# Folding the memory keys into the query weights of a cross-attention, with the logits' second half as seven products of quarters

## The chip, the cores and the metric

The kernel runs on one core of one Trainium2 chip. The metric is the device time of one execution in microseconds (us), the median of several runs. The trace comes from the hardware profiler, for one execution.

## The reference

One layer of a streaming encoder over 1024 rows of 1024 numbers, in fp32: a mixing part with two groups of eight attention heads, a cross-attention with four heads into 256 memory rows, and a feed-forward part, each between two RMS norms. The change concerns the cross-attention and what lies around it:

```
def memory_cross_attention(h, mem_n, w_mq, w_mk, w_mv, w_mo):
    B, S, _ = h.shape
    M = mem_n.shape[1]
    q = (h @ w_mq).reshape(B, S, MEM_HEADS, MEM_HEAD_DIM)
    k = (mem_n @ w_mk).reshape(B, M, MEM_HEADS, MEM_HEAD_DIM)
    v = (mem_n @ w_mv).reshape(B, M, MEM_HEADS, MEM_HEAD_DIM)
    logits = jnp.einsum('bshd,bmhd->bhsm', q, k).astype(jnp.float32) * (MEM_HEAD_DIM ** -0.5)
    p = jax.nn.softmax(logits, axis=-1).astype(v.dtype)
    o = jnp.einsum('bhsm,bmhd->bshd', p, v).reshape(B, S, D_MODEL)
    return o @ w_mo
```

`h` is the RMS norm (gain `g_mem_pre`) of the rows behind the mixing part, `mem_n` that of the memory rows. Four heads of 256 dimensions, and 256 memory rows, so that the logits of one row are 1024 numbers.

## The kernel before

All products are made in three matmuls (`mm3`, L174 to L176): each factor is split into a high part, rounded to a shorter format, and a low part, which is the rest, and high x high, high x low and low x high are added in PSUM. In the names, `hi` and `lo` (or `h` and `l`) are these parts. ScalarE (ACT) makes the high part with a copy (L321 for the weights) and VectorE (DVE) or GpSimd the low part with a subtraction (L327, L330). Each matmul takes 128 rows by 128 columns of weights and 512 or 256 columns.

The order of the instructions is written by a planner, `Flow` (L56). Each engine (V, S, G, D for DVE, ACT, GpSimd and DMA issues) has a time at which it is next free; each instruction is put with a cost and a call that follows it; the products come as generators of steps, each with its cost on TensorE (PE) and a condition on tokens (`free`, buffers) and marks (`seen`, results). What the planner decides is the program order of each engine; on the chip each engine runs in that order and waits on semaphores. Loads and stores are issued by SyncE (SP), also in that order; the planner counts 0.55 us for the issue of one and a fixed time (2.5 to 6 us) until it is there.

The first phase (`attention_phase`, L1507) runs the attention of the mixing part, and fills PE's time with `filler_steps`: the projections of queries, keys and values, then `memory_key_steps` (`mk`, whose results are kept on the chip as `km`), then the output projection's first half, `mix_steps(0)`, and `memory_value_steps` (`mv`). `mix_steps` needs the attention output: a class `Outputs` (L947) loads it from DRAM (`oin<-od`, L995, four loads for 512 columns of one group), ACT and DVE split it (`yT_hi` L989, `yT_lo` L990), ACT squares it (L992) and DVE adds the squares into `sq` (L970), and `rstd_steps` (L1003) transposes the sums on PE (`ssh`, L1016), from which the group's row norms come. The products `yw` leave PSUM through ACT (`yt`, L1146, with the norm `rs` as scale) and go to DRAM (`yd`, L1148). In the names of this stage the first digit is the half of the tokens and the second the group: `oin100`, `oin010` and `oin110` follow one another, and `ssh01` belongs to `oin010`.

The second phase has `mix_steps(1)`, then the rows: `close_row` (L1061) adds the residual, takes the norm (DVE L1091 multiplies the row by its norm and by the gain `g_mem_pre`), and stores `x1d`; `row_steps` transposes and splits the rows (`h2T`). `query_steps` (L1213, `mq`) makes the queries, `memory_score_steps` (L1240, `ms`) the logits, per head, half of the tokens and block of 128 rows, with the largest value by a reduction on DVE (L1256), the exponential on ACT (L1258), and the division by the sum (L1261). `memory_turn_steps` transposes the probabilities, `memory_out_steps` multiplies by the values, and `product_quarters` and `product_steps` make the product with `w_mo`, the first half of the tokens in seven products of quarters (sums `wt` of `w_mo`, made ahead, stored and reloaded). The feed-forward part follows. Weights are loaded by `Stock` (L260) in a fixed list of blocks of 512 KB (`wraw`), when a raw buffer is free, and split when a home (`w`, `wq`, `u4`) is free.

## Time and profile before

| | us |
|---|---|
| median of 3 runs | 1451.21 (1451.16 to 1451.9) |
| the profiled execution | 1451.39 |
| its span in the trace | 1449.6 |
| PE busy | 1441.1 |
| DVE busy | 964.9 |
| ACT busy | 822.9 |
| GpSimd (POOL) busy | 386.6 |

The span is what the trace covers, from the first to the last recorded instruction; the execution took 1.8 us more. In a row of groups the columns are: line, engine, operation, output <- inputs, shape, count | busy us, mean ns of one | idle time of the engine just ahead of them, and what ended it. A timeline's row begins with the start and the length in us. PE clock is the share of full speed that the throttle granted. The DMA share is the mean busy share of the core's 16 DMA engines.

### The profile page before, as it was taken

To read this page: it belongs to the slowest core of one execution; us is meant where nothing else is said; L and a number is where in the kernel's file an instruction comes from. 1 tells how busy PE (TensorE), PEld (TensorE's weight loads), DVE (VectorE), ACT (ScalarE), POOL (GpSimd) and SP (SyncE) were. 2 spreads that over 40 slices of the span, in tenths; PEclk is the share of its full clock that TensorE was granted. 3 is DMA by queue.
4 is the path that set the end of the run, shared out by engine and by line. 5 is a ranking of instruction groups with operands and counts; after the bars stand their busy time and mean duration, and the time that the engine had idled before them with its cause. 6 is when DMAs were issued, how large, how long until landed. Compare 5 with 4: busy or idle time off the path is not lost.

```text
span 1449.6 us, 20870 instructions
## 1 busy us (share of the span) xinstructions
PE 1441.1 (99%) x7236; PEld 1220.1 (84%) x7236; DVE 964.9 (67%) x1650; ACT 822.9 (57%) x1466; POOL 386.6 (27%) x458
## 2 busy tenths in 40 slices
PE   9999999999999999999999999999999999999998
PEld 9888888888889888888888888888888888888886
DVE  5577778867667556966685697665555766655576
ACT  7457776666577664566665455545555453444442
POOL 1345555444344202300021504333331000000021
PEclk9999999999999999999999999999999999999999
DMA  8233567855538766542362646754444875445565
GB/s 336 69 100 92 145 166 192 276 124 126 131 95 246 217 211 234 190 156 71 118 204 71 206 159 233 262 180 160 160 157 163 299 302 197 136 148 187 185 251 203
DMA packets 100970, 259.44 MB, mean 179 GB/s; under 512 B 12520, under 2 KB 25072, under 8 KB 100864
## 3 DMA queue, kind: packets, MB, share of 16 engines
q1 hardware_dynamic: 96112, 249.71, 51.1%
q0 software_dynamic: 4608, 8.39, 4.1%
q8 instruction: 57, 0.93, 0.3%
q14 instruction: 49, 0.40, 0.1%
q10 hardware_dynamic: 144, 0.00, 0.0%
HBM read 181.98 MB, written 76.08 MB: 178 GB/s over the span
## 4 chain that ended last, share of the span: by engine, by line
PE 98%; DMA 0%; ACT 0%; DVE 0%; SPq 0%; issue 0%; DVEq 0%; POOLq 0%; POOL 0%; ACTq 0%
PE pv L636 4%; PE fx L175 4%; PE fx L174 4%; PE fx L176 4%; PE ptr L586 4%; PE px L176 3%; PE fy L174 3%; PE fy L175 3%; PE px L175 3%; PE px L174 3%; PE fy L176 3%; PE q L174 2%; PE q L175 2%; PE q L176 2%; PE mq L174 2%; PE yw L174 2%
## 5 line engine op out<-in xcount | busy, mean ns | idle before, releaser
L592 DVE TENSOR_TENSOR p<-ptr,p 128x512 fp32r<-128x512 f32 (+1 forms) x152 | 92.4, 616 | 31.6 <-ACT p L595 30.5
L2103 ACT ACTIVATE whif<-ra 128x1024 fp32r<-128x1024 f32 x37 | 39.2, 1061 | 127.0 <-PE fy L175 62.6
L2105 DVE TENSOR_TENSOR wlof<-ra,whif 128x1024 fp32r<-128x1024 f32 x37 | 45.3, 1225 | 89.4 <-ACT whif L2103 89.3
L595 ACT ACTIVATE p<-ptr 128x512 fp32r<-128x512 f32 (+1 forms) x152 | 79.8, 538 | 43.2 <-PE ptr L586 42.3
L2217 POOL TENSOR_SCALAR rf<-sf 128x1 f32<-128x1 f32 x8 | 8.3, 1032 | 324.7 <-ACT jf L2202 324.4
L636 PE MATMUL pv<-p,vs 128*128 128x512 f32 (+1 forms) x304 | 86.7, 372 | 0.0
L174 PE MATMUL fx<-vhif,whif 128*128 128x512 f32 x168 | 65.4, 389 | 0.0
L175 PE MATMUL fx<-vlof,whif 128*128 128x512 f32 x168 | 65.4, 389 | 0.0
L176 PE MATMUL fx<-vhif,wlof 128*128 128x512 f32 x168 | 65.4, 389 | 0.0
L636 PEld LDWEIGHTS pv<-p,vs 128*128 128x128 f32 x304 | 53.4, 189 | 8.7 <-DVE p L592 0.2
L1992 POOL TENSOR_TENSOR sc<-wf,wf 128x512 f32<-128x512 f32 x14 | 22.1, 1576 | 142.5 <-DMA wf<-in_w_ff 117.6
L174 PE MATMUL k<-hT_hi,whik 128*128 128x512 f32 x128 | 52.5, 411 | 0.0
L174 PE MATMUL mq<-h2T_hi,whimq 128*128 128x512 f32 x128 | 51.6, 403 | 0.0
L174 PE MATMUL q<-hT_hi,whiq 128*128 128x512 f32 x128 | 51.0, 398 | 0.0
L174 PE MATMUL yw<-whiwo,yT_hi 128*128 128x512 f32 x128 | 50.6, 395 | 0.0
L175 PE MATMUL k<-hT_lo,whik 128*128 128x512 f32 x128 | 50.2, 392 | 0.0
L176 PE MATMUL k<-hT_hi,wlok 128*128 128x512 f32 x128 | 50.2, 392 | 0.0
L175 PE MATMUL mq<-h2T_lo,whimq 128*128 128x512 f32 x128 | 50.1, 391 | 0.0
L175 PE MATMUL q<-hT_lo,whiq 128*128 128x512 f32 x128 | 50.1, 391 | 0.0
L176 PE MATMUL mq<-h2T_hi,wlomq 128*128 128x512 f32 x128 | 50.0, 391 | 0.0
L176 PE MATMUL q<-hT_hi,wloq 128*128 128x512 f32 x128 | 50.0, 391 | 0.0
L645 ACT ACTIVATE ot<-pv 128x512 f32<-128x512 f32 x64 | 37.8, 593 | 21.3 <-PE pv L636 21.1
(673 smaller groups left out, 4951.7 us busy)
## 6 DMA issues: line engine op xcount, KB each, us to landing
ra<-gd SPq DMA_DIRECT2D x56, 512.0 KB, 3.5
wg<-in_w_ff SPq DMA_DIRECT2D x56, 512.0 KB, 4.9
wf<-in_w_ff SPq DMA_DIRECT2D x38, 512.0 KB, 4.2
gd<-s SPq DMA_DIRECT2D x48, 256.0 KB, 2.1
od<-ot SPq DMA_DIRECT2D x64, 128.0 KB, 2.7
od<-od POOLq DMA_DIRECT2D x32, 256.0 KB, 4.9
wrawmq<-in_w_mq SPq DMA_DIRECT2D x16, 512.0 KB, 4.1
gd<-u SPq DMA_DIRECT2D x32, 256.0 KB, 2.0
```

The costliest lines, as they stand in the source:

```text
L174: nc.tensor.matmul(ps, lh, rh, start=start, stop=False, skip_group_check=more)
L175: nc.tensor.matmul(ps, lh, rl, start=False, stop=False, skip_group_check=more)
L176: nc.tensor.matmul(ps, ll, rh, start=False, stop=stop, skip_group_check=more)
L586: nc.tensor.transpose(tr[:, m, :], sp[:, k * P:(k + 1) * P], ident)
L592: flow.put("V", at, 0.56 if dead else 0.7, lambda: nc.vector.tensor_sub(pl[:, live, :], tr[:, live, :], f(ph[:, live, :])), done)
L595: flow.put("S", flow.end, 0.49 if dead else 0.6, lambda ph=ph, tr=tr, live=live: nc.scalar.activation(ph[:, live, :], tr[:, live, :], AF.C ...
L636: nc.tensor.matmul(pv[:, :, q0 * P:(q0 + k1 - k0) * P], v, x[:, :, k0:k1, :].rearrange("p m k q -> p m (k q)"), start=c == 0 and m == 0, s ...
L645: nc.scalar.activation(box["t"][:, :, :, ::step], pv.rearrange("p m (k q) -> p m k q", q=P), AF.Copy)
L1992: eng.tensor_sub(sc[:, k1], r0[:, k0], r1[:, k0])
L2103: nc.scalar.activation(ah, ra, AF.Copy)
L2105: nc.vector.tensor_sub(al, ra, f(ah))
L2217: nc.gpsimd.tensor_scalar(r, ssf[b][:, 0:1], ssf[b][:, 1:2], EPS, op0=ALU.add, op1=ALU.add)
```

## The change

The logits of a row are h (w_mq k^T) for each head, so the product of the query weights and the memory keys is made once, for 1024 x 1024 numbers (4 heads x 256 memory rows), and the rows are multiplied with it. The new `fold_steps` runs in the first phase between the keys and `mix_steps(0)`: it loads `w_mq` in transposed blocks, multiplies each with `km` (tiles `fm`), ACT scales the result by `gm` (the gain `g_mem_pre` times 1/16), ACT and DVE split it (`fh`, `fl`), and SP stores both parts to DRAM: 16 stores of 512 KB (L945 of the changed file). GpSimd makes four sums of quarters (T1 to T4), 8 more stores of 512 KB (L925). The second phase loads them again: the parts directly into their homes (`Stock.direct`), the sums raw and split as before.

The rows are no longer multiplied by their norm: `close_row` keeps the row itself (x1), its norm goes to `r2`, and the softmax takes it as the scale of the exponential. `query_steps` and `memory_score_steps` are gone. For the first half of the tokens `logit_steps` makes the logits for two heads at a time (512 columns). For the second half `logit_quarters` makes them in seven products of quarters (Strassen's way), from sums of quarters of the transposed rows (`quarter_rows`); parts of the results are copied from PSUM (ACT) and added to later ones (DVE). More probabilities are held (`mp` from 4 buffers to 8, `pt` from 1 to 2), the weights get two more homes (`wq`), and some low parts of `w_mo` are made on GpSimd.

```diff
+    mld = [[[dr.tile([P, 2, HT], F32, name=f"ml{pr}{kp}{m}") for m in "hl"] for kp in range(4)] for pr in range(2)]
+    mlt = {n: [dr.tile([P, 2, HT], F32, name=f"ml{n}{k}") for k in range(2)] for n in ("T1", "T2", "T3", "T4")}
+    ML = (("A11", lambda k: mld[0][k]), ("A12", lambda k: mld[0][2 + k]), ("S2", lambda k: mlt["T2"][k]),
+          ("S1", lambda k: mlt["T1"][k]), ("S3", lambda k: mlt["T3"][k]), ("S4", lambda k: mld[1][2 + k]),
+          ("A22", lambda k: mlt["T4"][k]))
+    FOLD = (0, 1, 4, 5, 2, 3, 6, 7)
...
+        def direct(self):
+            key, src, shape = self.to_load.pop(0)
+            home = self.home.get(key, "w")
+            for _ in range(1 + (home == "u4")):
+                free[home].take()
+            both = all_of(key, 2)
+
+            def load():
+                w = self.homes(key, shape)
+                for m in range(2):
+                    nc.sync.dma_start(f(w[m]), src[m])
+
+            flow.load(flow.now, load, lambda at: (both(at), both(at)), 6.0)
...
+    def fold_steps(keep):
+        km = keep.pop(0)
+        stored = all_of("folded", 24)
+        for k in range(2):
+            raw = {}
+
+            def after(at, k=k, raw=raw):
+                T = {"T1": (0, 0), "T3": (0, 1), "T2": (1, 1), "T4": (1, 0)}
+                steps = [("T1", (0, 1), (0, 0)), ("T3", (1, 1), (0, 1)), ("T2", (1, 1), (0, 0)), ("T4", (1, 0), (1, 1))]
+
+                def go(at, i=0):
+                    if i < 4:
+                        n, x, y = steps[i]
+                        d = raw[T[n]]
+
+                        def summed(end, n=n, d=d):
+                            flow.load(end, lambda: nc.sync.dma_start(mlt[n][k], d),
+                                      lambda e: (free["u4"].give(e), stored(e)), 3.0)
+                            go(end, i + 1)
+
+                        flow.put("G", at, 2.4, lambda: nc.gpsimd.tensor_sub(d, raw[x], raw[y]), summed, 1)
+
+                go(at)
+
+            summing = all_of(("fs", k), 4, after)
+
+            def split(at, a, pr, k=k, raw=raw, summing=summing):
+                box = {}
+
+                def hi():
+                    box["h"], box["l"] = (u4(f"f{m}{k}{a}{pr}", (P, 2, HT)) for m in "hl")
+                    nc.scalar.activation(box["h"], raw[a, pr], AF.Copy)
+
+                def done(end):
+                    summing(end)
+                    for m, x in enumerate("hl"):
+                        flow.load(end, lambda m=m, x=x: nc.sync.dma_start(mld[pr][a * 2 + k][m], f(box[x])),
+                                  lambda e: (free["u4"].give(e), stored(e)), 3.0)
+
+                flow.chain(at, [("S", 1.06, hi), ("V", 1.22, lambda: nc.vector.tensor_sub(
+                    box["l"], raw[a, pr], f(box["h"])))], done, 1)
+
+            for a in range(2):
+                part = {}
+                for pr in range(2):
+                    part[pr] = all_of(("fm", k, a, pr), 2, lambda end, a=a, pr=pr, split=split: split(end, a, pr))
+                for j in range(2):
+                    kc = a * 4 + k * 2 + j
+                    for pr in range(2):
+                        for h in range(2):
+                            yield (0.72, lambda: h or there(("mq", kc), "keyed") and (j or free["u4"].ready(3))
...
+                            for nb in range(2):
+                                c = pr * 4 + h * 2 + nb
+                                mm3(ps[:, h, :], wh[:, c, :], wl[:, c, :], km.hi(c), km.lo(c), nb == 0, nb == 1)
...
+                        flow.put("S", flow.end, 0.63, lambda kc=kc, d=raw[a, pr][:, j, :], ps=ps: nc.scalar.activation(
+                            d, ps.rearrange("p a b -> p (a b)"), AF.Copy, scale=gm[:, kc:kc + 1]),
+                            lambda at, bk=bk, one=part[pr]: (free[bk].give(at), one(at)), 1)
+                    stock.done(("mq", kc))
...
+            d = y if nm == "w" else x
+            nc.vector.scalar_tensor_tensor(d, y, r[0], x, op0=ALU.mult, op1=ALU.add)
 
         def store(end):
-            flow.load(end, lambda: nc.sync.dma_start(dst[n], xin[nm, n]), mark(("x1d", n)) if nm == "w" else None, 3)
+            if nm == "w":
+                free["xt"].give(end)
+                flow.load(end, lambda: nc.sync.dma_start(dst[n], y), mark(("x1d", n)), 3)
+
+                def inverse():
+                    c = r2[:, n:n + 1]
+                    nc.gpsimd.tensor_scalar(c, s2, EPS, None, op0=ALU.add)
+                    nc.gpsimd.tensor_tensor(c, c, mhalf[:, 0:1], op=ALU.pow)
+
+                flow.chain(end, [("S", 1.1, lambda: square_sum(y, s2)), ("G", 0.95, inverse)], reached(("r2", n)), 1)
+                return then(end)
...
-    def query_steps(th, first=0, last=8):
-
-        for h in range(4):
-            for nb in range(2):
-                for kc in range(KC if first <= h * 2 + nb < last else 0):
...
-                    wh, wl = stock.w["mq", th, h, nb]
-                    act = acts["h2", th]
-                    mm3(ps, wh[:, kc, :], wl[:, kc, :], act.hi(kc), act.lo(kc), kc == 0, kc == KC - 1)
...
-    def memory_score_steps():
-        for th in range(2):
-            for h in range(4):
-                for b in range(4):
...
-                    for nb in range(2):
-                        qh, ql = qm[th, h, nb]
-                        mm3(ps, qh[:, bs], ql[:, bs], km.hi(h * 2 + nb), km.lo(h * 2 + nb), nb == 0, nb == 1)
...
+    def logit_quarters():
+        X, Y, lg, sts = {}, {}, {}, {}
+        for p, (a, _) in enumerate(ML):
+            on = Y if p in (1, 3, 5) else X
+            tag, fresh = "s" if on is Y else "mm", p in (0, 1, 3)
+            for kp in range(2):
+                for tp in range(2):
...
+                    wh, wl = stock.w["ml", 1, p, kp]
+                    ah, al = lq[a]
+                    c = slice(tp * P, tp * P + P)
+                    flat = on[tp].rearrange("p a b -> p (a b)")
+                    for j in range(2):
+                        mm3(flat, ah[:, kp * 2 + j, c], al[:, kp * 2 + j, c], wh[:, j, :], wl[:, j, :],
+                            fresh and kp == 0 and j == 0, kp == 1 and j == 1, not fresh)
+                    if tp == 1:
+                        stock.done(("ml", 1, p, kp))
+                    if kp == 1:
+                        logits_leave(p, tp, on[tp], tag, lg)
...
+    def logit_steps(th, prs=(0, 1)):
+
+        for pr in prs:
+            ps = {}
+            order = [(kp, b) for bs in ((0, 1), (2, 3)) for kp in range(2) for b in bs] if th == 0 and pr == 0 \
+                else [(kp, b) for kp in range(2) for b in range(4)]
+            for kp, b in order + [(kp, b) for kp in (2, 3) for b in range(4)]:
+                tag = "mm" if b < 2 else "s"
+                yield (1.362, lambda: there(("ml", th, pr, kp), ("h2", "T", th, b // 2 * 2, kp * 2)) and (
+                    (kp or free[tag].ready()) and (kp < 3 or free["mp"].ready())))
+                act = acts["h2", th]
+                if kp == 0:
+                    free[tag].take()
+                    ps[b] = mm_tile([P, 2, NM], f"ms{th}{pr}{b}", tag)
+                wh, wl = stock.w["ml", th, pr, kp]
+                c = slice(b * P, (b + 1) * P)
+                flat = ps[b].rearrange("p a b -> p (a b)")
+                for j in range(2):
+                    kc = kp * 2 + j
+                    mm3(flat, act.hi(kc, c), act.lo(kc, c), wh[:, j, :], wl[:, j, :], kc == 0, kc == KC - 1)
+                if b == 3:
+                    stock.done(("ml", th, pr, kp))
+                if kp == 3:
+                    soft(th, pr, b, ps[b], tag)
...
+        def exp(h):
+            def call():
+                if h == 0:
+                    box["p"] = p2x.tile([P, 2, NM], F32, tag="mp", bufs=8, name=f"mp{th}{pr}{b}")
+                    for k in range(2):
+                        pm[th, pr * 2 + k, b] = box["p"][:, k, :]
+                nc.scalar.activation(box["p"][:, h, :], ps[:, h, :], AF.Exp, scale=rr, bias=st[:, h:h + 1],
+                                     accum_out=st[:, 2 + h:3 + h])
+            return call
...
     def second_filler():
         yield from mix_steps(1)
-        yield from query_steps(0)
-        yield from query_steps(1, 0, FIRST)
+        yield from logit_steps(0)
+        yield from logit_quarters()
         yield from product_quarters()
-        yield from query_steps(1, FIRST)
         yield from product_steps(1, (0,))
 
     def second_rows():
         yield from row_steps("w", 0, "h2", "h2T")
-        yield from row_steps("w", 1, "h2", "h2T")
+        yield from quarter_rows()
         yield from row_steps("m", 0, "h3", "h3T")
...
         yield from memory_key_steps(keep)
+        yield from fold_steps(keep)
         seen["keys"] = flow.end
         yield from mix_steps(0)
         yield from memory_value_steps(keep)
```

How the instructions now stand: first SP, at the end of the attention, where `yd` are the stores of the first output products and `oin01` the attention output's loads. Before:

```order
L995 DMA oin101_6268<-od3_1_94 128x512
L1148 DMA yd0_103<-yt000_6299 128x512
L652 DMA od7_1_102<-ot712_6320 64x2x256
L654 DMA od7_1_102<-ot712_6320 64x256
L1148 DMA yd1_104<-yt001_6343 128x512
L1148 DMA yd2_105<-yt002_6375 128x512
L652 DMA od7_1_102<-ot713_6389 64x2x256
L654 DMA od7_1_102<-ot713_6389 64x256
L1148 DMA yd3_106<-yt003_6402 128x512
L1148 DMA yd0_103<-yt010_6421 128x512
L995 DMA oin010_6444<-od4_0_95 128x512
```

And of the change, from the same load to the same one (`ml` are the stores of the folded parts, `mlT` those of the sums, `wrawmv` loads of the memory value's weights):

```order
L1101 DMA oin101_6654<-od3_1_96 128x512
L319 DMA wrawmv_0_1_6675<-in_w_mv 128x1024
L925 DMA mlT20_158<-fm011_6424 128x1024
L925 DMA mlT40_162<-fm010_6398 128x1024
L945 DMA ml03h_146<-fh110_6670 128x1024
L945 DMA ml03l_147<-fl110_6671 128x1024
L945 DMA ml13h_154<-fh111_6680 128x1024
L319 DMA wrawmv_0_2_6719<-in_w_mv 128x1024
L945 DMA ml13l_155<-fl111_6681 128x1024
L1266 DMA yd0_105<-yt000_6688 128x512
L925 DMA mlT11_157<-fm100_6484 128x1024
L1266 DMA yd1_106<-yt001_6715 128x512
```

Seven stores and two loads of 512 KB now stand between the last load of `oin101` and the first of `oin010`; the last stores of the attention output (`od7`) have moved up to the fold's first stores.

Second ACT, where the split of the attention output (`yT_hi`) and the evacuations of the products (`yt`) follow one another. Before:

```order
L1146 ACTIVATE yt010_6421<-yw0010_6404,rs00_4619 128x512
L1146 ACTIVATE yt011_6456<-yw0011_6429,rs00_4619 128x512
L1146 ACTIVATE yt012_6474<-yw0012_6458,rs00_4619 128x512
L989 ACTIVATE yT_hi010_6439<-oin010_6444,gcol_84 128x512 x2
L989 ACTIVATE yT_hi011_6440<-oin011_6445,gcol_84 128x512
L1146 ACTIVATE yt013_6491<-yw0013_6475,rs00_4619 128x512
```

And of the change:

```order
L1264 ACTIVATE yt010_6800<-yw0010_6779,rs00_4647 128x512
L1095 ACTIVATE yT_hi010_6740<-oin010_6745,gcol_84 128x512 x2
L1095 ACTIVATE yT_hi011_6741<-oin011_6746,gcol_84 128x512 x2
L1098 ACTIVATE sq01_6744<-oin010_6745 128x512
L1264 ACTIVATE yt011_6840<-yw0011_6802,rs00_4647 128x512
L1098 ACTIVATE oin010_6745<-oin010_6745 128x512
L1098 ACTIVATE oin011_6746<-oin011_6746 128x512 x2
L1264 ACTIVATE yt012_6864<-yw0012_6845,rs00_4647 128x512
L1095 ACTIVATE yT_hi110_6808<-oin110_6813,gcol_84 128x512 x2
L1095 ACTIVATE yT_hi111_6809<-oin111_6814,gcol_84 128x512
L1264 ACTIVATE yt013_6886<-yw0013_6867,rs00_4647 128x512
```

The split of `oin010` has moved ahead of the evacuation of `yw0011`, and that of `oin110`, which came behind the evacuation of `yw1010`, ahead of that of `yw0013`.

Third PE, where the transposes of the squares' sums stand. Before:

```order
L176 MATMUL yw1002_6537<-whiwo_0_0_1_6240,yT_lo101_6265 128x512
L1016 MATMUL ssh01_6563<-ident_76,sq01_6443 128x128 x4
L174 MATMUL yw1003_6570<-whiwo_0_0_0_6110,yT_hi100_6262 128x512
L175 MATMUL yw1003_6570<-wlowo_0_0_0_6111,yT_hi100_6262 128x512
L176 MATMUL yw1003_6570<-whiwo_0_0_0_6110,yT_lo100_6264 128x512
```

And of the change:

```order
L176 MATMUL yw1000_6889<-whiwo_0_0_0_6622,yT_lo100_6650 128x512
L1125 MATMUL ssh01_6902<-ident_76,sq01_6744 128x128 x4
L174 MATMUL yw1000_6889<-whiwo_0_0_1_6643,yT_hi101_6649 128x512
L175 MATMUL yw1000_6889<-wlowo_0_0_1_6644,yT_hi101_6649 128x512
L176 MATMUL yw1000_6889<-whiwo_0_0_1_6643,yT_lo101_6651 128x512
```

`ssh01` stood behind the product `yw1002` and now stands within `yw1000`, 30 matmuls of this projection earlier.

273 lines of the change are left out of this document (208 added, 65 removed).

## The prediction

> **What bounds the kernel now.** I read the page first: the span, the busy shares, the granted clock and the chain that ended last.
>
> ```profile
> span 1449.6 us, 20870 instructions
> PE 1441.1 (99%) x7236; PEld 1220.1 (84%) x7236; DVE 964.9 (67%) x1650; ACT 822.9 (57%) x1466; POOL 386.6 (27%) x458
> PEclk9999999999999999999999999999999999999999
> PE 98%; DMA 0%; ACT 0%; DVE 0%; SPq 0%; issue 0%; DVEq 0%; POOLq 0%; POOL 0%; ACTq 0%
> ```
>
> TensorE is busy for 99% of the span, the chain lies on it for 98%, and no slice shows a throttled clock. So a matmul taken out is worth its full interval, and any new wait of PE costs its full length. The view of waits, for PE alone, says that there is hardly any wait yet:
>
> ```profile
> PE sc6g L513 <- DVE mnc6g L517: 1.2, 1, 1.2
> PE warm L1529 <- DVE mhalf L194: 1.0, 1, 1.0
> ```
>
> (total us, times, longest). The sum therefore needs two numbers: the matmuls that go, and the waits that come.
>
> **The matmuls.** The groups by line give what is removed: all products `mq` and `ms`.
>
> ```profile
> L174 PE MATMUL mq<-h2T_hi,whimq 128*128 128x512 f32 x128 | 51.6, 403 | 0.0
> L175 PE MATMUL mq<-h2T_lo,whimq 128*128 128x512 f32 x128 | 50.1, 391 | 0.0
> L176 PE MATMUL mq<-h2T_hi,wlomq 128*128 128x512 f32 x128 | 50.0, 391 | 0.0
> ...
> L174 PE MATMUL ms<-km_hi,qh 128*128 128x256 f32 x64 | 18.1, 283 | 0.0
> L176 PE MATMUL ms<-km_hi,ql 128*128 128x256 f32 x64 | 18.1, 283 | 0.0
> L175 PE MATMUL ms<-km_lo,qh 128*128 128x256 f32 x64 | 18.1, 283 | 0.0
> ```
>
> The means (390 and 283 ns) overlap in the pipeline; what a matmul costs is the distance between starts, from the timeline of PE:
>
> ```profile
> 601.38 0.39 PE L174 MATMUL mq<-h2T_hi,whimq 128*128 128x512 f32 x1
> ...
> 602.06 0.39 PE L174 MATMUL mq<-h2T_hi,whimq 128*128 128x512 f32 x1
> ...
> 615.09 0.28 PE L174 MATMUL ms<-km_hi,qh 128*128 128x256 f32 x1
> ...
> 615.45 0.28 PE L174 MATMUL ms<-km_hi,qh 128*128 128x256 f32 x1
> ```
>
> Three starts lie 0.68 us apart, so 512 columns cost 0.227 us; 256 columns cost 0.36 / 3 = 0.12. Removed: 384 x 0.227 + 192 x 0.12 = 110.2 us. Added: the fold, 8 blocks x 8 pieces x 3 = 192 of 256 columns, 23.0 us; logits of the first half of the tokens, 2 pairs of heads x 4 row blocks x 8 x 3 = 192 of 512 columns, and of the second half seven products x 2 x 2 x 2 x 3 = 168 of 512 columns, together 360 x 0.227 = 81.7. The transposes stay 32 for 32. Net: 24 matmuls of 512 columns, **-5.45 us**; the program on PE is shorter by just 24 rows (6963 to 6939).
>
> **The stores of the fold.** This is the part that I think decides. The folded keys do not stay on the chip: 16 stores (L945) and 8 of quarter sums (L925), 512 KB each, 12.6 MB in all, are issued by SP beside the loads of the output projection's and the memory value's weights, `oin` and `yd`. What this costs the 16 DMA engines, I take from windows in which they were full (last two columns: their busy share, GB/s), and from the page's list of issues (KB, median us to landing):
>
> ```profile
> 10.00:20.00 10.00, 10.00 (x85) 1.00 1.03 415
> 540.00:550.00 10.00, 10.00 (x47) 1.00 1.02 390
> 1000.00:1010.00 10.00, 10.00 (x46) 1.00 0.61 203
> ```
>
> ```profile
> od<-od POOLq DMA_DIRECT2D x32, 256.0 KB, 4.9
> wtT<-wm SPq DMA_DIRECT2D x8, 512.0 KB, 3.8
> oin<-od SPq DMA_DIRECT2D x16, 256.0 KB, 4.2
> yd<-yt SPq DMA_DIRECT2D x16, 256.0 KB, 2.5
> ```
>
> At 415 GB/s 512 KB are 1.26 us of all engines; at 390, with loads and stores mixed, 1.34; at 203 / 0.61 = 333, 1.57. I take 1.30, between the two full windows, and 0.65 for 256 KB. `wtT<-wm` lands 3.8 us after its issue of which 1.3 is moving; I count 1.2 us ahead of the first packet and 1.0 behind the last (estimates: they leave 0.3 for a queue).
>
> Where it lies in time: I add the intervals of PE's rows in program order. By that count the first `yw` of before stands at 473.3, and the trace has it at 484.0:
>
> ```profile
> L174 PE MATMUL yw<-whiwo,yT_hi x47: 387/389/478, 484.0 to 519.8; 128*128 128x512 f32 x47
> ```
>
> So the span's time is the count plus 10.7. In the changed program the fold ends at 499.4 + 10.7 = 510.1, its first store is issued near 495.0 (behind copy, split and subtraction of the first two blocks), and from there SP's queue goes on with hardly a gap. PE comes to the transposes `ssh01`, which are to give the row sums of the second group for the first half of the tokens, at 523.0 + 10.7 = **533.7** if nothing waits. Ahead of them on ACT stand `yT_hi010` and the first `yT_hi110`, on DVE the first `yT_lo110` ahead of the last sum into `sq01`. So `ssh01` needs the first load of `oin110`, the ninth of those twelve.
>
> Engine work from the first store up to that load: 24 stores, 3 weight blocks `wo` and 3 `mv`, 30 x 1.30 = 39.0; 9 `oin` and 4 `yd`, 13 x 0.65 = 8.45; two accumulations `od<-od` and one `ot`, 2.35 (an estimate, 0.9 and 0.55, from their 256 and 128 KB). Together 49.8 us. 495.0 + 1.2 + 49.8 + 1.0 = 547.0. Behind the landing come three instructions, each once:
>
> ```profile
> L989 ACT ACTIVATE yT_hi<-oin,gcol 128x512 fp32r<-128x512 f32 x16 | 10.6, 713 | 0.0
> ...
> L990 DVE SCALAR_TENSOR_TENSOR yT_lo<-oin,gcol,yT_hi 128x512 fp32r<-128x512 f32 x16 | 11.4, 748 | 11.7 <-ACT yT_hi L989 7.8 <-issue 3.8
> ...
> L970 DVE TENSOR_TENSOR sq<-sq,oin 128x512 f32<-128x512 f32 x12 | 8.8, 731 | 2.4 <-ACT oin L992 2.0
> ```
>
> 0.71 + 0.75 + 0.73 = 2.2, so `ssh01` starts at 549.2 rather than 533.7: **+15.5 us**. At 415 GB/s it is 14.2, at 390 17.0, at 333 25.3. Below, nothing: the load takes 4.2 us in before, and SP issues it in time.
>
> PE does not lose it in one piece. ACT has `yT_hi100` ahead of `yt001`, in the order it cannot leave, and `yw0003` needs the PSUM bank that `yt001` empties: by the same queue `oin100` lands near 522, and PE stands some 5 us there, then again further on. In before `yT_hi` never stands: its rows follow without idle time.
>
> ```profile
> 490.74 1.33 ACT L989 ACTIVATE yT_hi<-oin,gcol 128x512 fp32r<-128x512 f32 x2
> 491.99 0.69 ACT L1146 ACTIVATE yt<-yw,rs 128x512 f32<-128x512 f32 x1
> ```
>
> `ssh11` comes 7 us of matmuls later and needs the last `oin` 2 us after the first of its set, so it does not wait again; with the stores through, the loads for the second projection find a free queue.
>
> The Trainium skill, page "DMA: Bandwidth & Descriptors", section Bandwidth, sets the limit of HBM for one core at about 358 GB/s; by it the stall would be an estimated 21 us. The window at 415 GB/s is over that, so here the measurement decides.
>
> **The second phase.** Eight DVE passes go:
>
> ```profile
> L1091 DVE SCALAR_TENSOR_TENSOR yw<-xtw,rw,g_mem_pre 128x1024 f32<-128x1024 f32 x8 | 10.2, 1279 | 1.5 <-POOL rw L1042 1.5
> ...
> L1258 ACT ACTIVATE mp<-ms,mst 128x256 f32<-128x256 f32 x32 | 15.0, 471 | 15.0 <-DVE mst L1256 15.0
> ```
>
> They lie beside PE's mixing products, so their 10.2 us are worth nothing. The softmax keeps 32 exponentials of 471 ns, now in pairs, with the row's norm as their scale. The quarter sums of the second half are needed only after the first half's 192 products (44 us). Of the folded weights 36 loads of 512 KB come with 8 splittings, where 16 loads with 16 splittings were; 36 x 1.30 = 47 us of the engines, spread over some 100 us. I cost this at 0; if a pair of exponentials stands late before a bank is free, 0 to +2.
>
> **The sum.** 1451.39 (the profiled execution, 1.8 over its span) - 5.45 + 15.5 = 1461.4; the median of the runs shown is 0.2 lower than that execution, so 1461.2.
>
> **Rivals.**
> - *The stores are hidden; faster.* `ssh01` stands late only if the engines' work ahead of that load exceeds 533.7 - 2.2 - 1.0 - 496.2 = 34.3 us; I count 49.8. If writing and reading ran side by side in the engines, only the larger direction would count: 24 stores, 4 `yd` and the accumulations, some 36 us, a stall of 1 to 2; with a little less, none. Time: 1446 to 1447.5. For it: SP's DMAs are asynchronous, and no engine waits for a store of the fold itself before the second phase. Against it: the window at 540 has both kinds and is full at 390.
> - *Half hidden; the same.* If the queue runs at some 80% of the counted work (40 us), 5 to 6 us are lost and the gain of PE is eaten: 1449 to 1454.
> - *The queue is slower.* 333 GB/s, the lowest rate of the rows, gives 1451.2 - 5.45 + 25.3 = 1471; half way to it 1466.
> - *PE is slow after it has stood.* At the start, after idling, PE's work runs at half pace:
>
> ```profile
> 1.05 3.78 PE L1529 MATMUL warm<-ones 128*128 128x128 f32 x16 [1.05 <-DVE mhalf L194]
> 4.87 1.18 PE L1634 MATMUL v<-whiv,hT_hi 128*128 128x264 f32 x4
> 5.89 0.64 PE L1634 MATMUL v<-whiv,hT_lo 128*128 128x264 f32 x4
> ```
>
> Four matmuls of 264 columns take 1.02 us from start to start and then 0.48, though the granted clock reads full. Over the first 4.8 us the loss is about half, 2.4 us. A stand of 5 us could bring it back once behind `ssh01`: 1461.2 + 2.4 = 1463.6. No row shows a stand this long later on; PE's longest was 1.2 us. The Trainium skill, page "TensorE: Matmul & The Clock Gate", Part 1, has the array fall to half rate after an idle window of about 3.4 us, which speaks for this rival.
>
> **How the numbers follow.** Within 0.2% (2.9 us, about what a measurement of this kernel can tell from no change) is 1448.3 to 1454.1. Chances: the forecast 0.50 (1458 to 1463), PE slow after it 0.10, the slower queue 0.08, half hidden 0.09, hidden 0.23. Half hidden and the forecast's own spread give 0.08 for the same; faster 0.24, slower 0.68. The likeliest is 1461.2, its own range 1458 to 1466. The range must reach to the hidden case: 1446 to 1467.
>
> **What would show it.** PE's busy time falls by about 5; its idle time grows to some 15 us between 515 and 550, laid to ACT `yt` and to `sq`. `oin` lands 10 to 20 us after issue where it was 4.2, and ACT's idle time ahead of `yT_hi` goes to the DMA of `oin`. The windows from 495 to 545 show a DMA share near 1.0 and about 400 GB/s. If `oin` lands within 8 us and PE stays at 99%, the stall is wrong; if the share is at 1.0 and PE still does not wait, my chain on ACT and DVE is wrong; if PE waits at `ms` or `mtr` after 600, the second phase was costed too low.

## The result, and the profile after

| | before | after |
|---|---|---|
| median of 4 runs, us | 1451.33 (1451.16 to 1451.9) | 1485.88 (1485.38 to 1486.85) |
| profiled execution, us | 1451.39 | 1485.38 |
| its span, us | 1449.6 | 1483.6 |
| mean granted clock of PE | 0.999 | 0.991 |

The changed kernel is slower by 34.6 us: the ratio is 1.0238, with a 95% interval of 1.022 to 1.0256. The prediction said slower, at 1461.2 in a range of 1446 to 1467; the sign was right and the size was less than a third of what came.

The page of the changed kernel, with the rows that stood first in the prediction (span, busy time of the engines, granted clock in 40 slices, chain that ended last):

```profile
span 1483.6 us, 21007 instructions
PE 1445.7 (97%) x7212; PEld 1221.4 (82%) x7212; DVE 966.3 (65%) x1636; ACT 839.5 (57%) x1488; POOL 448.9 (30%) x499
PEclk9999999999999989999999999999999999999999
PE 39%; DVE 1%; DMA 0%; ACT 0%; issue 0%; DVEq 0%; POOLq 0%; POOL 0%; ACTq 0%
```

PE has the 24 matmuls less that were counted (7236 to 7212), and yet its busy time is 4.6 us longer, where the prediction had it fall by about 5: matmuls at a lower clock count as busy for longer. One slice, the stage of the fold, shows that clock. The chain covers only 40% of the span: followed back from the end, it leaves PE where a product of the feed-forward part waits half a microsecond for DVE, and breaks off near 884 us. So it says nothing of the stages that the change touches, and the view of PE's waits has to be read (releaser; total us, times, longest):

```profile
PE rt L1923 <- DVE vs L1954: 8.8, 1, 8.8
PE yw L174 <- ACT yt L1264: 7.7, 3, 3.2
PE yw L175 <- DVE wlowo L355: 5.6, 2, 5.3
PE tr_h3T L1315 <- DVE ym L1209: 4.0, 1, 4.0
PE ssh L1125 <- DVE sq L1076: 1.5, 1, 1.5
```

Before, the two longest entries were 1.2 and 1.0. Three places wait: one near the start of the program (`rt`), one in the stage of the fold (`yw`, `ssh`), and one late in the second phase (`tr_h3T`). For what each is worth, two marks that both programs pass are set against each other: the last `mv` product ends the first phase's filler, and the first `px` with `wah` begins the feed-forward part. The groups by tile, before (last figures: first and last start, us):

```profile
L176 PE MATMUL mv<-whimv,mT_lo x32: 389/389/397, 532.5 to 554.1; 128*128 128x512 f32 x32
L174 PE MATMUL px<-h3T_hi,wah x4: 389/389/478, 831.0 to 833.1; 128*128 128x512 f32 x4
```

and after:

```profile
L176 PE MATMUL mv<-whimv,mT_lo x32: 388/389/390, 587.7 to 608.7; 128*128 128x512 f32 x32
L174 PE MATMUL px<-h3T_hi,wah x4: 393/398/476, 863.0 to 865.1; 128*128 128x512 f32 x4
```

| stretch | before | after | difference | of which matmuls | lost |
|---|---|---|---|---|---|
| start to the last `mv` | 554.1 | 608.7 | +54.6 | fold +23.0 | 31.6 |
| last `mv` to first `px` | 276.9 | 254.3 | -22.6 | -110.2 + 81.7 = -28.5 | 5.9 |
| first `px` to the end | 618.6 | 620.6 | +2.0 | 0 | 2.0 |

The sum of the differences is 34.0, that of the spans. The matmuls give the 5.5 that they were to give, and 39.5 us are lost: 31.6 in the first phase (10.6 of it at its start, as the first experiment shows, so 21.0 in the stage of the fold), 5.9 in the second, 2.0 behind it. The trace of that experiment, without the loss at the start, agrees: its last `mv` stands at 598.5, and 598.5 - 554.1 - 23.0 = 21.4.

The stage of the fold is read from the windows, as in the prediction (us; busy time and count of PE, PE's loads, DVE, ACT and POOL; granted clock, DMA share, GB/s). After:

```profile
510.00:520.00 10.00, 10.00 (x86) 10.00 (x85) 6.36 (x4) 9.50 (x13) 5.58 (x5) 1.00 1.03 395
520.00:530.00 10.00, 4.44 (x18) 3.03 (x16) 10.00 (x5) 5.29 (x7) 9.92 (x5) 0.83 1.04 385
530.00:540.00 10.00, 6.86 (x29) 5.37 (x29) 8.81 (x5) 2.83 (x4) 8.70 (x3) 1.00 1.04 380
540.00:550.00 10.00, 9.85 (x37) 7.65 (x38) 8.56 (x9) 5.79 (x10) 3.57 (x4) 0.83 1.03 415
550.00:560.00 10.00, 5.49 (x17) 3.77 (x16) 2.77 (x4) 4.65 (x8) 0.94 (x1) 0.83 1.02 399
```

The queue is full throughout at 380 to 415 GB/s, as was foreseen, and PE stands in it. But from 520 to 540 DVE and GpSimd are busy nearly all the time too, DVE with five instructions in each ten microseconds, GpSimd with five and then three: a possible second limit that the prediction had not seen.

One profile below is not read: the profiled execution of the fifth experiment was disturbed (2061.47 us at a granted clock of 0.654), so only the times of its other three runs are given.

### The profile page after: what moved, and what is told of

Its sections match the earlier page's. It is cut to its first block, busy times and chain, and to the rows that moved or that the text cites. A ratio compares the mean times of both kernels' runs of the same rounds, so it can differ in the third digit from the quotient of the medians.

```text
span 1483.6 us, 21007 instructions
## 1 busy us (share of the span) xinstructions
PE 1445.7 (97%) x7212; PEld 1221.4 (82%) x7212; DVE 966.3 (65%) x1636; ACT 839.5 (57%) x1488; POOL 448.9 (30%) x499
## 2 busy tenths in 40 slices
DMA packets 108460, 286.20 MB, mean 193 GB/s; under 512 B 13481, under 2 KB 26033, under 8 KB 108353
## 5 line engine op out<-in xcount | busy, mean ns | idle before, releaser
L175 PE MATMUL yw<-wlowo,yT_hi 128*128 128x512 f32 x128 | 51.7, 404 | 5.6 <-DVE wlowo L355 5.6
L176 PE MATMUL yw<-whiwo,yT_lo 128*128 128x512 f32 x128 | 51.4, 401 | 0.0
L175 PE MATMUL fy<-vlof,whif 128*128 128x512 f32 x128 | 49.8, 389 | 0.0
L174 PE MATMUL fy<-vhif,whif 128*128 128x512 f32 x128 | 49.8, 389 | 0.0
```

The source lines that it names most:

```text
L174: nc.tensor.matmul(ps, lh, rh, start=start, stop=False, skip_group_check=more)
L175: nc.tensor.matmul(ps, lh, rl, start=False, stop=False, skip_group_check=more)
L176: nc.tensor.matmul(ps, ll, rh, start=False, stop=stop, skip_group_check=more)
```

## The experiments

All times are medians in us, with the range of the runs and the ratio to the kernel before, run on the same chip (1450.98 to 1451.59). The changed kernel itself is 1485.88.

| run | made from | time | ratio, 95% |
|---|---|---|---|
| e1_gm_late | changed | 1475.32 (1474.62 to 1475.73) | 1.0168 [1.0151, 1.0185] |
| e2_gm_alone | before | 1462.8 (1461.76 to 1463.84) | 1.0082 [1.0062, 1.0102] |
| e3_sums_dve | e1 | 1475.14 (1474.43 to 1475.29) | 1.0166 [1.0151, 1.0181] |
| e4_half | e1 | 1467.71 (1465.55 to 1469.44) | 1.0115 [1.01, 1.013] |
| e5_half_dve | e1 | 1460.87 (1459.9 to 1461.48) | 1.0062 [1.0046, 1.0079] |
| e6_fold_behind | e1 | 1475.23 (1474.99 to 1475.67) | 1.0164 [1.0149, 1.0179] |
| e7_before_cover | before | 1460.85 (1460.62 to 1460.9) | 1.0064 [1.0047, 1.0081] |
| e8_behind_dve | e6 | 1474.92 (1473.44 to 1475.62) | 1.016 [1.0145, 1.0175] |
| e9_wloa_pool | e1 | 1475.84 (1474.82 to 1476.98) | 1.0169 [1.0154, 1.0184] |
| e10_before_stores | before | 1467.53 (1467.05 to 1468.45) | 1.0112 [1.0095, 1.0129] |
| e11_half_dve_wloa | e5 | 1462.39 (1461.39 to 1463.59) | 1.0077 [1.0062, 1.0092] |
| e12_sums_later | e3 | 1462.51 (1460.67 to 1464.72) | 1.0076 [1.0057, 1.0094] |
| e13_splits_behind | e12 | 1464.21 (1463.76 to 1464.93) | 1.0089 [1.0074, 1.0104] |
| e14_stores_spread | e13 | 1466.63 (1465.14 to 1467.02) | 1.0103 [1.0086, 1.012] |

### The start: one small operation ahead of the row norms

The changed kernel loads the gain `gm` at the start and scales it on GpSimd. The timeline of GpSimd there (start, length, operation, idle time before), after:

```profile
32.29 0.27 POOL L1985 TENSOR_SCALAR gm<-gm 128x8 f32<-128x8 f32 x1 [13.02 <-DMA gm<-in_g_mem_pre]
32.65 0.24 POOL L1910 TENSOR_SCALAR rall<-ss 128x4 f32<-128x4 f32 x1
```

and before:

```profile
22.10 0.24 POOL L1607 TENSOR_SCALAR rall<-ss 128x4 f32<-128x4 f32 x1 [2.95 <-ACT junk L1601]
```

The scaling takes 0.27 us, but it stands in GpSimd's order ahead of `rall`, the norms of the first rows, and waits 13.0 us for its load, which SP issues only at 25.2, behind the first rows and weights, and which lands 7.0 us later. `rall` starts 10.55 us later, and through DVE's `vs` PE waits 8.8 at `rt`. The first experiment moves only that operation.

```diff
         nc.sync.dma_start(gm, t["g_mem_pre"])
-        nc.gpsimd.tensor_scalar(gm, gm, 0.0625, None, op0=ALU.mult)
...
         d = root(1)
+        nc.gpsimd.tensor_scalar(gm, gm, 0.0625, None, op0=ALU.mult)
```

> The scaling of the gain gm on GpSimd is moved in the program from ahead of the first row norms (rall) to behind the second; nothing else changes. Theory P: GpSimd stood 13.0 us for the small load of gm, and with it rall, the values and PE (8.8 us in one wait, slow matmuls behind it): the time falls by 9 to 11 us, to about 1475 to 1477. Rival: the stage at 40 us has slack behind it, and the loss is made up before the fold: the time stays within 2 us of 1485.9.

It gave back 10.6 us (1485.88 to 1475.32), and the wait at `rt` is gone. The second puts the load and the scaling alone into the kernel before, at the same place.

```diff
+    gm = const.tile([P, KC], F32, name="gm")
...
+        nc.sync.dma_start(gm, t["g_heads"])
+        nc.gpsimd.tensor_scalar(gm, gm, 0.0625, None, op0=ALU.mult)
```

> The kernel before, with nothing added but a load of 128x8 numbers behind gcol and their scaling on GpSimd at the place that the change gives them (the result is not used). Theory P: 1451.3 + 9 to 11 = 1460 to 1462. Rival (the wait comes from something else in the change): within 1 us of 1451.3.

It costs 11.8 us, 0.8 over the range expected, and the waits of PE in its trace show the same place:

```profile
PE rt L1621 <- DVE vs L1652: 9.1, 1, 9.1
```

Both directions agree: 8 numbers per partition, 0.27 us of work, cost 10.6 to 11.8 us. All later runs made from the changed kernel have the first edit.

### The stage of the fold: stores, or two engines in each other's way

DVE's timeline of the changed kernel in the stage:

```profile
517.23 6.20 DVE L948 TENSOR_TENSOR fl<-fm,fh 128x1024 fp32r<-128x1024 f32 x2 [1.49 <-ACT fh L940]
523.35 6.67 DVE L355 TENSOR_TENSOR wlowo<-wrawwo,whiwo 128x1024 fp32r<-128x1024 f32 x2
```

Two subtractions take 6.2 us there, 3.1 each. The other theory is the queue. The third run makes the sums of quarters on DVE instead of GpSimd; the fourth stores only half of each tile of the folded weights and leaves the engines' work as it is. The second phase then loads that half twice, so the bytes loaded stay and only those stored are halved: the trace of this run moves 279.91 MB, that of e1 286.20, which is 24 x 0.262 MB less. Half of the folded weights are missing from the result.

```diff
-                        flow.put("G", at, 2.4, lambda: nc.gpsimd.tensor_sub(d, raw[x], raw[y]), summed, 1)
+                        flow.put("V", at, 1.22, lambda: nc.vector.tensor_sub(d, raw[x], raw[y]), summed, 1)
```

> As e1, with the eight sums of quarters T1 to T4 made on DVE rather than on GpSimd; the stores are the same. Theory Q (the bytes queued on the DMA engines set when oin lands): within 2 us of e1, since the stores and their number stay. Theory C (GpSimd's sums slow the DVE subtractions beside them from 1.2 to 3.3 us, and these delay wlowo and fl): the PE wait for wlowo of 5.3 us and its consequence go, 4 to 8 us less than e1.

```diff
-                nc.sync.dma_start(raw, src)
+                nc.sync.dma_start(raw, src[:, 0:1].to_broadcast([P, 2, HT]) if key[0] == "ml" else src)
...
-                    nc.sync.dma_start(f(w[m]), src[m])
+                    nc.sync.dma_start(f(w[m]), src[m][:, 0:1].to_broadcast([P, 2, HT]))
...
-                            flow.load(end, lambda: nc.sync.dma_start(mlt[n][k], d),
+                            flow.load(end, lambda: nc.sync.dma_start(mlt[n][k][:, 0], d[:, 0]),
...
-                        flow.load(end, lambda m=m, x=x: nc.sync.dma_start(mld[pr][a * 2 + k][m], f(box[x])),
+                        flow.load(end, lambda m=m, x=x: nc.sync.dma_start(mld[pr][a * 2 + k][m][:, 0], f(box[x])[:, 0]),
```

> As e1, but each of the 24 stores of the fold moves half its tile (256 KB), and the loads of the second phase read that half twice, so the second half of the folded weights is wrong in value and the compute is the same in kind and count. Theory Q: 24 x 0.65 = 15.6 us less in the queue ahead of oin, so 12 to 16 us less than e1. Theory C: DVE and GpSimd do the same, so within 3 us of e1. A mix lies between.

The sums on DVE changed nothing (1475.14 for 1475.32), though they did what they were to do. The groups of DVE (busy us, mean ns of one | idle before), of the changed kernel:

```profile
L948 DVE TENSOR_TENSOR fl<-fm,fh 128x1024 fp32r<-128x1024 f32 x8 | 18.2, 2304 | 5.8 <-ACT fh L940 5.7
L355 DVE TENSOR_TENSOR wlowo<-wrawwo,whiwo 128x1024 fp32r<-128x1024 f32 x8 | 14.9, 1869 | 5.6 <-ACT whiwo L336 5.6
```

and of e3_sums_dve:

```profile
L948 DVE TENSOR_TENSOR fl<-fm,fh 128x1024 fp32r<-128x1024 f32 x8 | 10.1, 1278 | 4.4 <-ACT fh L940 4.3
L355 DVE TENSOR_TENSOR wlowo<-wrawwo,whiwo 128x1024 fp32r<-128x1024 f32 x8 | 9.7, 1223 | 13.1 <-ACT whiwo L336 13.1
```

The subtractions are at their usual 1.2 us again, and the wait for them is nearly gone; another one has grown in its place (PE's waits, e3_sums_dve):

```profile
PE yw L174 <- ACT yt L1264: 15.0, 2, 10.0
PE yw L175 <- DVE wlowo L355: 1.5, 1, 1.5
```

With half the bytes it is the other way round (PE's waits, e4_half):

```profile
PE yw L175 <- DVE wlowo L355: 5.3, 2, 5.0
...
PE yw L174 <- ACT yt L1264: 3.9, 1, 3.9
```

`yt` falls and `wlowo` stays. That gave 7.6 us (1475.32 to 1467.71), between what the two theories expected. So two limits seem to stand side by side, each covering what the other would give. The fifth run takes both away.

> As e1, with both edits of e3 and e4: the eight sums on DVE and half the bytes of each of the 24 stores (the second half of the folded weights wrong in value, compute the same). Theory of two limits side by side: e3 took the wait for wlowo away but let the sums' stores into the queue sooner, e4 shortened the queue but left that wait; together they take away most of what either leaves, 14 to 20 us less than e1, 1455 to 1461. Rival, that the queue alone counts: as e4, 1466 to 1469.

It gives 14.4 us against e1, where the two alone gave 0 and 7.6: behind the stores stands the slowing of the two engines, and the other way round. The eleventh run, below, has both edits, one more, and a trace: `yt` waits 4.1 there and `wlowo` 1.5. What half the bytes give lies in this stage: the last `mv` of e4 stands at 592.0, 6.5 us ahead of that of e1, and from there to the first `px` the two traces differ by 0.4.

The tenth run puts stores alone, the same 24 of 512 KB, into the kernel before, one per microsecond ahead of the output projection, with no fold and no sums.

```diff
+    scr = [dr.tile([P, 4, 256], F32, name=f"scr{i}") for i in range(24)]
...
+        for i in range(24):
+            flow.load(flow.end + 1.0 * i, lambda i=i: nc.sync.dma_start(scr[i], f((mem_in[2].h + mem_in[2].l)[i % 4])))
         seen["keys"] = flow.end
```

> The kernel before, with nothing added but 24 stores of 512 KB from the normed memory tiles (mT) to a scratch in DRAM, issued by SP from the end of the memory keys on at 1 us distance in the planner; nobody waits for them but the release of mT. Theory Q: 19 of them stand ahead of the second group's oin in the queue: 19 x 1.30 + 13 x 0.65 + 3.5 = 36.7 us of the engines from 484.3 on, so oin011 lands near 522, ssh01 starts near 524 rather than 517.7: 4 to 9 us over before. Theory C (what was lost in the change is the engines' work around the fold, not the queue): within 1.5 us of before.

It costs 16.3 us (1451.2 to 1467.53), so the stores are enough by themselves; it is also far more than the 4 to 9 expected of them. ACT's timeline shows through what (e10_before_stores):

```profile
506.37 0.69 ACT L1147 ACTIVATE yt<-yw,rs 128x512 f32<-128x512 f32 x1 [5.03 <-DMA yd<-yt]
512.04 0.69 ACT L1147 ACTIVATE yt<-yw,rs 128x512 f32<-128x512 f32 x1 [4.98 <-DMA yd<-yt]
523.22 2.11 ACT L990 ACTIVATE yT_hi<-oin,gcol 128x512 fp32r<-128x512 f32 x3 [10.49 <-DMA oin<-od]
```

The loads `oin`, the prediction's path, are late, and so are the stores `yd`, which it had only counted as bytes: `yt` cannot leave PSUM before an older `yd` has freed its buffer. The two are one chain: SP issues the `oin` for which ACT waits 10.49 us only at 514.16, right behind the `yd` that stores the `yt` of 512.04. The expectation had counted bytes alone.

If the place of the stores decides, they need not be fewer. The twelfth run keeps all bytes, but issues the eight sums' stores 34 us (in the planner's time) later, behind the loads.

```diff
-                            flow.load(end, lambda: nc.sync.dma_start(mlt[n][k], d),
+                            flow.load(end + 34, lambda: nc.sync.dma_start(mlt[n][k], d),
```

> As e3 (gm moved, sums on DVE), with the eight stores of the sums issued 34 us later in the planner's time, so that they stand among and behind the loads of the second group's oin and the stores yd rather than ahead of them; the bytes and the number of stores are the same. Theory Q (what stands ahead in the queue decides): 8 x 1.30 = 10 us less ahead of oin and yd, the stage loses 8 to 12 us less, 1463 to 1467. Rival from e6 (the stores cost their time wherever they stand in this stretch): within 3 us of e3, 1472 to 1478.

It gives 12.6 us against e3, nearly what half the bytes gave with the sums on DVE. The windows of e12_sums_later, in the stage:

```profile
510.00:520.00 10.00, 6.35 (x29) 4.73 (x28) 8.06 (x8) 5.05 (x7) 0.82 (x1) 1.00 1.04 373
520.00:530.00 10.00, 9.10 (x33) 7.12 (x34) 7.43 (x9) 7.71 (x13) 0.00 (x0) 0.83 1.04 395
530.00:540.00 10.00, 9.91 (x46) 8.01 (x45) 2.71 (x4) 2.77 (x4) 1.24 (x2) 1.00 1.02 401
```

The queue is as full as ever, and from 530 on PE hardly stands: in this stage the place of these stores in the order is worth about as much as their bytes. The fourteenth run went on in this way (the last four `ml` stores 15 us later, the sums at a lower rank) and lost 2.4 us against e13. PE's wait for `yt` grows from 3.2 to 6.0; ACT no longer waits for a `yd`, but 5.4 us for an `oin`, whose loads SP issues 3 us later than in e13, behind two of the `ml` stores. Which of the two edits did this was not separated.

```diff
-                        flow.put("V", at, 1.22, lambda: nc.vector.tensor_sub(d, raw[x], raw[y]), summed, 1)
+                        flow.put("V", at, 1.22, lambda: nc.vector.tensor_sub(d, raw[x], raw[y]), summed, 3)
...
-                        flow.load(end, lambda m=m, x=x: nc.sync.dma_start(mld[pr][a * 2 + k][m], f(box[x])),
+                        flow.load(end + (15 if k == 1 and a == 1 else 0.0), lambda m=m, x=x: nc.sync.dma_start(mld[pr][a * 2 + k][m], f(box[x])),
```

> As e13, with four more stores (the last two pairs of folded blocks) 15 us later in the planner's time, and the sums behind the other work of DVE. Theory Q: with oin100 and the first yd stores ahead of them, the last wait for yt (3.0 us) and that for wlowo (1.5 us) shrink: 3 to 6 us less than e13, 1452 to 1457, about the kernel before. Rival (the queue is now full for as long anyway, and the yd stores, which free the buffers of yt, land late as they do in e10): within 1.5 us of e13, or slower.

Two runs moved the whole fold behind `mix_steps(0)`, with the sums on GpSimd and, by the edit of the third run, on DVE.

```diff
-            self.blocks += [(("mq", kc), t["w_mq"][kc], [P, KC, P]) for kc in FOLD]
             pair = [P, 2, HT]
             self.blocks += [(("wo", 0, nh, i), row_pair(t["w_out"], i, nh), pair) for nh in range(2) for i in range(2)]
+            self.blocks += [(("mq", kc), t["w_mq"][kc], [P, KC, P]) for kc in FOLD]
...
-        yield from fold_steps(keep)
         seen["keys"] = flow.end
         yield from mix_steps(0)
+        yield from fold_steps(keep)
         yield from memory_value_steps(keep)
```

> As e1, with the fold moved behind the first half of the output projection (mix_steps(0)), its weights' loads behind those of that projection, and the loads of oin allowed as soon as the keys are there; the 24 stores stay. Theory: the oin loads stand ahead of the stores in SP's queue and land in 4 to 6 us, PE's waits for yt, wlowo and ssh go, and the stores drain beside mv and the second half of the projection; some waits for buffers come in their place: 12 to 20 us less than e1, 1455 to 1463. Rival, that the stores cost their time wherever they stand (then yw, xtw and wo loads are late): within 5 us of e1.

> As e6, with the eight sums on DVE. If GpSimd's sums slow DVE's subtractions where the fold now stands, 2 to 5 us less than e6; if the queue or the buffers decide there, within 1.5 us of e6.

Neither gained (1475.23 and 1474.92), against the 12 to 20 us expected of the first. The waits move with the fold (PE's waits, e6_fold_behind):

```profile
PE mv L174 <- ACT whimv L336: 5.6, 3, 2.7
PE fm L176 <- POOL wlomq L358: 3.7, 2, 2.9
PE mv L175 <- DVE wlomv L355: 2.2, 4, 0.8
```

`ssh` and `yw` no longer wait; the splits of the next weights do, whose loads now stand among and behind the stores (ACT waits 18.5 us for loads of `wrawmv`). So here an order that suits one stage costs as much in the next.

### The second phase: `tr_h3T`

`tr_h3T` needs the first half's rows behind the memory product, and the second half's product lies beside that chain. DVE's order has weight splits of the feed-forward part (`wlo_a`) between its steps. The ninth run gives one to GpSimd, the eleventh does so on top of the fifth.

```diff
-            was[j] = HiLo(raw, D, wp, "w", 2, f"a{j}").both(nc.vector)
+            was[j] = HiLo(raw, D, wp, "w", 2, f"a{j}").both(nc.gpsimd if j == 1 else nc.vector)
```

> As e1, with the low part of the second weight block of the feed-forward part (wlo_a of block 1) made on GpSimd rather than on DVE, so that the subtraction no longer stands in DVE's order ahead of the last normed row ym03, for which tr_h3T waits 3.9 us. Theory: that subtraction waits for the load of wf, DVE stands behind it 1 us and works 2 us, while ym03 could be made at 822.0 and is at 825.5: the wait falls by 3 to 3.5 us and the time by 3 to 6 us (with the slow start behind it). Rival: something else is late at the same time (the products of the last rows, GpSimd): within 1 us of e1.

> As e5 (gm moved, sums on DVE, half the bytes of each store, so the second half of the folded weights wrong in value), with the edit of e9. If the causes add up: e5 less what e9 takes from e1, 1455 to 1458. Its profile shows what is left of PE's waits between 510 and 560.

Neither helped: `tr_h3T` waits 4.7 and 3.6, where it was 3.9 in e1, and the medians are 0.5 and 1.5 us longer than those of e1 and e5 (0.5 lies within the range of the runs). The thirteenth lets these splits stand where the code writes them.

```diff
-    for j in range(EARLY):
-        split_ahead(j, ff1_raw(j), j == 0)
+    with tc.manual_schedule():
+        for j in range(EARLY):
+            split_ahead(j, ff1_raw(j), j == 0)
```

> As e12, with the first three weight blocks of the feed-forward part (loads, high and low parts) put behind the whole second phase in the program's order, so that on DVE the last normed row ym03 and on ACT the squares ahead of it stand before them; nothing is left out. Theory O (in e9 the wait only moved from DVE to ACT, because whi_a, which waits for the load of wf, stood ahead of the squares there): tr_h3T's wait falls from 3.2 us to under 1.5 and the time by 3 to 6 us, 1457 to 1460. Rival (the chain of the last rows is simply longer than the product that covers it): the wait stays over 2.5 us, the time within 1.5 us of e12.

PE's waits in e13_splits_behind:

```profile
PE ym L174 <- DVE h3T_lo L1322: 4.2, 1, 4.2
PE tr_h3T L1315 <- DVE ym L1209: 2.1, 1, 2.1
```

In e12, its base, `tr_h3T` waits 3.2 and this `ym` 0.5. So the splits held `tr_h3T` by about 1.1 us. The rest may be the chain of the last rows itself, which no run isolates. The wait moves to `h3T_lo`, and the kernel is not faster (1464.21 for 1462.51, and the ranges overlap). The seventh run asked from the other side whether cover is missing. The kernel before keeps half of the second half's queries for the place between the quarters and the product (`FIRST`); this moves them ahead of the quarters, and the loads of their weights with them, as the list of blocks goes by `FIRST` too.

```diff
-    FIRST = 4
+    FIRST = 8
```

> The kernel before, with all eight query products of the second half of the tokens ahead of product_quarters (FIRST = 8 rather than 4), so that, as in the change, no query products stand between product_quarters and product_steps; nothing else changes. Theory of the lost cover: the wait of tr_h3T for the normed rows of the memory product (4 us and a slow start of PE behind it in the change) appears in this kernel too, 3 to 8 us over before. Rival (that wait comes from the splits moved to GpSimd or from the weights' loads of the change): within 1.5 us of before.

The kernel before becomes 9.5 us slower, 7.8 of it between the last `mv` and the first `px` (553.4 to 838.1), so what stands at this place is worth much, as cover or through the order of the loads. But its waits are others (PE's waits, e7_before_cover):

```profile
PE ms L174 <- ACT mp L1258: 2.4, 2, 2.1
PE ym L174 <- ACT mp L1258: 1.1, 1, 1.1
```

`tr_h3T`, for which the theory expected a wait, does not wait here. So this does not show that lost cover makes it wait in the change. That stays open, as do the 2.0 us behind the first `px`, of which the trace shows 0.7 as waits.

No version beats the kernel before; the best with all of the computation (e5 and e11 leave half of the stores out) is e12_sums_later at 1462.51, 0.76% slower.

## Why the prediction was wrong in size

- **The matmuls** (-5.45): right. 24 rows fewer, and the stretch from the last `mv` to the first `px` comes out as their count plus one wait.
- **What was not in the sum at all** (0, measured 10.6): the walk through the queues. The working followed SP, ACT, DVE and PE at the fold, and never GpSimd at the start, where the change added one small operation that waits for a new load. The diff shows it and the order on GpSimd would have shown `rall` behind it; a load's price stood in the prediction's own rows (3.8 us and more). This is the larger of the two failures in the first phase, and e1 and e2 settle it. It is not the only one: without it the time is 1475.32 (e1), still over the range.
- **The stores of the fold** (+15.5, measured 21.0): the mechanism was right, the term mis-sized. The predicted start of `ssh01`, 549.2, is 559.8 with the 10.6 us of the start; it began here (PE's timeline, after):

```profile
565.79 0.66 PE L1125 MATMUL ssh<-ident,sq 128*128 128x128 f32 x4 [1.54 <-DVE sq L1076]
```

  6.0 us later. All of it lies ahead of the landing of the load that the prediction named, the first of `oin110` (ACT's timeline, after):

```profile
563.63 2.05 ACT L1095 ACTIVATE yT_hi<-oin,gcol 128x512 fp32r<-128x512 f32 x3 [1.67 <-DMA oin<-od]
```

  The predicted landing is 547.0 + 10.6 = 557.6, and ACT's wait ends at 563.63; the three instructions behind it take the 2.2 us that were counted. The first store is issued at 505.36 (predicted 495.0 + 10.6 = 505.6). From there to 563.63 the engines were full (DMA share 1.01) and moved 22.0 MB at 378 GB/s. The term had 49.8 us at 512 KB in 1.30 us, which is 20.1 MB at 403 GB/s. So both factors were short: there were more bytes ahead of that load and beside it (two weight loads of 512 KB, issued at 503.78 and 504.93, were still to move in large part), and the rate was lower (395 in the mean of the five full windows, 214 in the first 5 us). The other waits of the stage, for the buffers that the stores `yd` hold and for DVE's slowed subtractions, and the lower clock behind each of them, lie ahead of `ssh01` and are part of the same 21 us: PE stands another 1.5 us at `ssh01` after all of them, and in e3, where the subtractions are fast again, the time is the same. Of the 21.0 us the trace shows 15.2 as waits in this stage; the other 5.8 are what is left. Three windows at a clock of 0.83 make 5.1 us of full speed, so most of it can be matmuls at a lower clock.
- **"`oin` lands 10 to 20 us after issue"**: wrong, and for a reason that matters. The landing of `oin`, after (us):

```profile
DMA to landing us min/median/max: 4.7/7.1/9.4
```

  The delay lies ahead of the issue, on SP (timeline of SP, after; start, length of the issue):

```profile
523.37 1.45 SPq L925 DMA_DIRECT2D mlT<-fm  x1
524.91 1.41 SPq L945 DMA_DIRECT2D ml11h<-fh  x1
526.41 1.24 SPq L945 DMA_DIRECT2D ml11l<-fl  x1
```

  One issue takes 1.2 to 1.5 us there, as long as the transfer of 512 KB at 400 GB/s (1.3), where the weight loads of the same size ahead of the fold's stores (503.78, 504.93) were issued in 0.33 each. Behind a full queue SP issues at the queue's own pace, and a load is late mostly because it has not been issued yet (its landing took 7.1 us in the median, for 4.2 before). The prediction's test for a stall that is not there was a landing within 8 us and PE at 99%. The median landing meets the first half, and only the second (PE at 97%) does not, so landing times alone would have misled: in e10 the longest landing is 8.9 us and ACT waits 10.49.
- **"Idle time of some 15 us, laid to `yt` and to `sq`"**: the waits between 494 and 609 are 15.2 us, as many as that, but the agreement is chance: `yt` has 7.7 and `sq` 1.5 of them, 5.6 are for DVE's `wlowo`, which was not foreseen, and the 5.8 lost beside them were in no term.
- **The second phase** (0, to +2; measured 5.9): too low. 4.0 are the wait at `tr_h3T`, whose cause stays open. The exponentials and the `ms` products, where a wait was thought possible, do not wait.
- **The rivals**: the hidden and the half-hidden case, 0.32 together, are gone: e10 prices the stores alone at 16.3 us. PE slow after it has stood was right, but it had been priced once, at 2.4; three of the five windows shown from 510 to 560 have a granted clock of 0.83, and up to 5.8 us may have gone with it. The slower queue was wrong: the full windows moved 380 GB/s and more, not 333.
- With the measured terms in place of the predicted ones: 1451.4 - 5.5 + 10.6 + 21.0 + 5.9 + 2.0 = 1485.4, the profiled execution. The terms are differences of the two traces, so they must add up; the sum shows where the time lies, not that each cause is understood.

## What to carry to other kernels

Where an engine runs in program order, each added operation has to be followed on its own engine's queue, small ones first: what counts is not its 0.27 us but what stands behind it while it waits. Stores for which nobody waits still hold up the loads and the buffers behind them in an issue queue (16.3 us for 24 of them here), and their order can be worth as much as their bytes: eight stores issued later gave 12.6 us with the DMA engines just as full and the sums on DVE. But putting them behind one stage is no gain where the next one needs its loads then (e6). Where removing one limit gives nothing, a second may stand just behind it, and only a run without both (0, 7.6 and 14.4 us here) tells what they hold.

## What the runs showed of the hardware

**DVE and GpSimd slow each other.** A DVE subtraction of 128 x 1024 fp32 numbers (`fl`) took 1.28 us with GpSimd free of sums (e3) and 2.30 on average with them beside it, with the DMA engines full in both; in the stretches where sums run all along, two take 6.2 to 6.7 us, 3.1 to 3.4 each; GpSimd's own sums took (groups by line, after)

```profile
L929 POOL TENSOR_TENSOR fm<-fm,fm 128x1024 f32<-128x1024 f32 x8 | 25.0, 3127 | 1.5 <-DVE fl L948 1.2
```

3.13 us on average, where the one subtraction of that size on GpSimd in the kernel before (`wlov`, at its start) took 2.40. The Trainium skill, page "GPSIMD Engine Reference", section 8, Key points, says that GpSimd shares its SBUF interfaces with VectorE and contends with DVE instructions that have two SBUF inputs. These runs agree, with a slowing of `fl` by 1.8 times on average.

**PE is slow after it has stood.** In e3_sums_dve, after a stand of 9.98 us (timeline of PE):

```profile
516.89 0.39 PE L176 MATMUL yw<-whiwo,yT_lo 128*128 128x512 f32 x1
527.25 0.80 PE L174 MATMUL yw<-whiwo,yT_hi 128*128 128x512 f32 x1 [9.98 <-ACT yt L1264]
527.85 0.63 PE L175 MATMUL yw<-wlowo,yT_hi 128*128 128x512 f32 x1
528.27 0.63 PE L176 MATMUL yw<-whiwo,yT_lo 128*128 128x512 f32 x1
...
533.31 0.40 PE L176 MATMUL yw<-whiwo,yT_lo 128*128 128x512 f32 x1
533.55 0.40 PE L174 MATMUL yw<-whiwo,yT_hi 128*128 128x512 f32 x1
```

From 527.85 on the starts lie 0.43 us apart, and from 533.55 on 0.23 again. From 527.25 to 533.31 there are 14 intervals, 6.06 us, which take 3.2 at the full pace of 0.227: one long stand cost 2.9 us beyond itself. The Trainium skill, page "TensorE: Matmul & The Clock Gate", Part 1, has half rate after at least one idle window of about 3.4 us, and full rate after at least one busy window of that length. The half rate agrees (0.43 us for 0.227), and the return took 6.06 us here, more than one such window and less than two.
